# Moving the first products of an expert layer's dense loop ahead, so that blocks without one come last

## The chip, the core and the metric

The kernel runs on one core of one Trainium2 chip. A core has five engines that run side by side and wait for each other through semaphores: TensorE (PE, matrix products; PEld is its weight load), VectorE (DVE), ScalarE (ACT), GpSimd (POOL) and SyncE (SP, which here issues DMA transfers). The metric is device time in microseconds for one execution; lower is better. Each engine works through its own list of instructions strictly in the order in which it was written, so an instruction that waits holds up everything behind it on its engine.

## The reference, cut to what matters

Two layers, each a token mixer (attention in the first, pooling in the second) followed by an expert layer. Nearly two thirds of the time goes to the loops of the two expert layers:

```python
def _peer(h, w_q, k1, k2, u_tab, v_tab):             # h: 512 tokens x 1024; tables: 16384 x 1024
    q = (h @ w_q).reshape(b, l, 8, 2, 128)           # 8 heads, two half queries
    s1, s2 = q[..., 0, :] . k1, q[..., 1, :] . k2    # scores against 128 keys each
    v1, i1 = top_k(s1, 16);  v2, i2 = top_k(s2, 16)
    top_s, pos = top_k(v1 + v2 (all pairs), 16)      # 16 experts of 16384 per head
    idx = i1 * 128 + i2 at pos;  g = softmax(top_s)
    a = gelu(u_tab[idx] . h)                         # 128 experts per token
    return sum(g * a * v_tab[idx])
x = layernorm(alpha * x + gate * _peer(...))
```

## The kernel before, in words

The 512 tokens of an expert layer are treated in two ways. For the first 384 tokens (`TD`, three tiles of 128) the kernel works densely: it goes through all 16384 experts in 128 blocks of 128. For block b the **first product** (`u_block`, L950) multiplies the block's rows of `peer_u` with the tokens, 24 matmuls 384 columns wide into PSUM tile `pA` or `pG`, and ScalarE writes the Gelu of it to a strip `gel[b]`. VectorE multiplies that strip by the block's gates (`w_mul`, L1134, result `W`; the gate is zero where a token did not choose the expert), `w_hi` and `w_lo` split `W` into a rounded part `WH` and a rest `WL`, and the **second product** (`v_block`, L1152) multiplies it with the block's rows of `peer_v`, 18 matmuls 512 columns wide, summed over all blocks in the PSUM tiles `acc`. Each half row block of a table is one transfer of 256 KB on SyncE's queue (`fetch`, tile `raw`, 6 buffers), and ScalarE (`hi`) and VectorE (`lo`, L101) split it in two as well (`prep`), four halves ahead of TensorE.

For the last 128 tokens the kernel **gathers**: `g_fetch` has GpSimd fetch, for all 128 tokens at once, the row of their i-th chosen expert (an indirect DMA of 512 KB into one of four slots of the tile `flat`), 128 rows of `peer_u`, then 128 of `peer_v`. `g_step` (L1260) has VectorE multiply a row of `peer_u` with the tokens and sum it (L1267), or add a row of `peer_v` to the sum `accg` (L1277). Before this can start, the choice of experts for these tokens must be made: `late_route` (L1384) does it in steps, on VectorE (`top16_steps`, `look_one`) and GpSimd (`ranks`, sums of `look_one`, the list `idx`). It is a Python generator; each `next(late)` writes the instructions of one more step, and four groups of two heads are done one after the other.

Before the loop stands a stretch in which the gates of the 384 tokens are made, while TensorE makes the first products of blocks 0 to 25 (`PRE + 2`). The gates go to DRAM and come back four blocks at a time (`g_load`, tile `gb`, 3 buffers, 768 KB).

The order is written out by hand (no scheduler moves anything): the loop over b from L1447 on. In the kernel before, iteration b makes the first product of block b + 3 (`LEAD`) if that is at least 26, so iterations 0 to 22 hold a second product alone, iterations 23 to 124 both, 125 to 127 a second alone. The strips of blocks 0 to 23 lie in the upper part of `flat` (`A0`); later ones use two buffers `gel`. One step of `late_route` is written per iteration up to 21, three from 22 on. `spread_rows` (L853) is a small planner: from estimated costs per iteration it works out up to which gathered row (`goal`) VectorE shall be after each iteration, from iteration 22 to 120. `Fin` loads what the closing layer norm needs; `last` (iteration 123) does it for the gathered tokens, `turn` (iteration 125) transposes that result in the first layer.

Of the kernel before, what the change touches and what calls it, by code (L numbers as in the profile page):

```python
# [10 lines left out]
F32 = mybir.dt.float32  # L11
# [25 lines left out]
TD = ND * 128  # L37
# [4 lines left out]
KB = 4  # L42
PRE = 24
# [8 lines left out]
def body(ctx: ExitStack, tc, A):  # L52
    nc = tc.nc
# [796 lines left out]
        return rt  # L850


    def spread_rows(pre, lead, begin, end):  # L853

        spec = []
        for b in range(end):
            u = pre + 2 <= b + lead < 128
            spec.append((4.12 + 4.15 * u, 2.5 + 1.4 * u, 2.05 + 1.48 * u))
        u = 0.5
        while True:  # L860
            x = [max(0.0, min((u * p - n) / 1.25, (0.95 * p - d) / 1.47)) if b >= begin else 0.0
                 for b, (p, n, d) in enumerate(spec)]
            if sum(x) >= 2 * NSEL:
                break
            u += 0.005
        goal, t = [], 0.0
        for v in x:
            t += v
            goal.append(min(2 * NSEL, int(t)))
        goal[-1] = 2 * NSEL  # L870
        return goal + [2 * NSEL] * (128 - end)
# [18 lines left out]
    def peer(rt):  # L890
# [5 lines left out]
        d1 = Pool("dense1", side=Y)  # L896
# [15 lines left out]

        NB = 128
        LEAD = 3
        GEND = 121
        seq = [("U", b, k) for b in range(PRE + 2) for k in range(2)]
        for b in range(NB):
            u = b + LEAD
            if PRE + 2 <= u < NB:
                seq += [("U", u, 0), ("U", u, 1)]  # L920
            seq += [("V", b, 0), ("V", b, 1)]
        pos_of = {k: i for i, k in enumerate(seq)}
        raw, HL = {}, {}
# [21 lines left out]
        gel, WHL, Wt = {}, {}, {}  # L945
        A0 = flat[:, 3 * 128 * SG:].rearrange("p (b t) -> p b t", b=PRE)

        def u_block(b, hook=None):
            p = psU.tile([128, 512], F32, name="pG" if b % 2 else "pA")
            for k in range(2):  # L950
                i = pos_of["U", b, k]
                fetch(i + 6)
                prep(i + 4)
                h_, l_ = HL.pop(i)
                for c in range(4):
                    cc, w = 4 * k + c, slice(c * 128, (c + 1) * 128)
                    mm3(p[:, :TD], (h_[:, w], l_[:, w]), (hH[:, cc, :], hL[:, cc, :]), cc == 0, cc == DC - 1)
                if k == 0 and hook:
                    hook()
            if b < PRE:  # L960
                gel[b] = A0[:, b, :]
            else:
                gel[b] = d1.tile([128, TD], F32, name="gel", bufs=2)
            nc.scalar.activation(gel[b], p[:, :TD], AF.Gelu)


# [254 lines left out]
        def g_load(j, queue):  # L1221
            if j < NB // KB:
                gb[j] = d2.tile([128, NSG, KB * SG], F32, name="gb", bufs=3)
                queue.dma_start(gb[j].rearrange("p s (i t) -> p s i t", t=SG), gates[l][:, :, KB * j:KB * (j + 1), :])
# [7 lines left out]
        def hook():  # L1232
            due[0] += per
            while due[0] >= 1.0:
                due[0] -= 1.0
                next(pipe, None)
# [14 lines left out]
        def g_fetch(n):  # L1251
            while step["f"] < min(n, 2 * NSEL):
                i = step["f"]
                assert i >= NSEL or i < step["n"]
                r = flat[:, i % 4 * D:(i % 4 + 1) * D]
                nc.gpsimd.indirect_dma_start(out=r, out_offset=None,  # L1256
                                             in_=A["peer_u_rows"] if i < NSEL else A["peer_v_rows"],
                                             in_offset=bass.IndirectOffsetOnAxis(ap=idx[:, i % NSEL:i % NSEL + 1], axis=0))
                rows[i] = r
                step["f"] += 1  # L1260
# [122 lines left out]
        def late_route():  # L1383

            at = [4 * D]

            def space(shape, dt=F32):
                n = math.prod(shape) * (2 if dt == BF else 4) // 4
                w = flat[:, at[0]:at[0] + n]
                at[0] += n  # L1390
                if dt != F32:
                    w = w.bitcast(dt)
                names = "abcd"[:len(shape)]
                return w.rearrange(f"p ({' '.join(names)}) -> p {' '.join(names)}", **dict(zip(names, shape)))

            V3, I3, Ib3 = space((2 * H, TK)), space((2 * H, TK), U32), space((2 * H, TK), BF)
            cand, T3, P3, pu3 = space((H, NC_)), space((H, TK)), space((H, TK), U32), space((H, TK), U32)
            f3, ab3, ids3 = space((4, 5, 2 * TK)), space((4, 2, 2 * TK), BF), space((4, 2, 2 * TK))
            x3, e3 = space((2, H * TK, TK), BF), space((2, H * TK, TK), BF)
            s3, E3 = space((1, H)), space((H, TK))  # L1400
            V4, Ib4 = [w.rearrange("p (h k) i -> p h k i", k=2) for w in (V3, Ib3)]
            x4, e4 = [w.rearrange("p k (h i) j -> p k h i j", h=H) for w in (x3, e3)]
            for g in range(H // 2):
                hs, ks = slice(2 * g, 2 * g + 2), range(4 * g, 4 * g + 4)
                for i, _ in enumerate(top16_steps([(V3[:, k], I3[:, k], S3[:, k]) for k in ks])):
                    if i % 5 == 4:
                        yield
                nc.scalar.copy(Ib3[:, 4 * g:4 * g + 4], I3[:, 4 * g:4 * g + 4])
                for k in range(2):
                    nc.scalar.copy(x4[:, k, hs], Ib4[:, hs, k, :, None].to_broadcast([128, 2, TK, TK]))  # L1410
                candidates(cand[:, hs], V4[:, hs, 0], V4[:, hs, 1], 2)
                yield
                for i, _ in enumerate(top16_steps([(T3[:, k], P3[:, k], cand[:, k])
                                                   for k in range(2 * g, 2 * g + 2)])):
                    if i % 5 == 4:
                        yield
                f, ab, id_ = [w[:, g].rearrange("p a (h k) -> p a h k", h=2) for w in (f3, ab3, ids3)]
                ranks(ab, P3[:, hs], pu3[:, hs], f)
                yield
                for k in range(2):  # L1420
                    look_one(id_[:, k], e4[:, k, hs], ab[:, k], x4[:, k, hs], 2)
                yield
                r = f3[:, g, 0]
                nc.gpsimd.tensor_scalar(r, ids3[:, g, 0], 128.0, float(l * NEXP), op0=OP.mult, op1=OP.add)
                nc.gpsimd.tensor_tensor(r, r, ids3[:, g, 1], op=OP.add)
                nc.gpsimd.tensor_copy(idx[:, 2 * g * TK:2 * (g + 1) * TK], r)
                step["n"] += 2 * TK
            nc.vector.tensor_tensor(E3, T3, T3[:, :, 0:1].to_broadcast([128, H, TK]), op=OP.subtract)
            nc.scalar.activation(E3, E3, AF.Exp)
            yield  # L1430
            nc.vector.reduce_sum(s3[:, 0], E3, axis=AX.X)
            nc.vector.reciprocal(s3[:, 0], s3[:, 0])
            nc.vector.tensor_tensor(ga.rearrange("p (h k) -> p h k", h=H), E3,
                                    s3[:, 0, :, None].to_broadcast([128, H, TK]), op=OP.mult)
# [6 lines left out]
            w_lo(b)  # L1441
        w_mul(2)
        late = late_route()
        first = PRE - 2
        goal = spread_rows(PRE, LEAD, first, GEND)
        fin = None
        for b in range(NB):  # L1447
            u = b + LEAD
            if b + 2 < NB:
                w_hi(b + 2)  # L1450
            if PRE + 2 <= u < NB:
                u_block(u)
            if b + 2 < NB:
                w_lo(b + 2)
            v_block(b)
            if b + 3 < NB:
                w_mul(b + 3)
                if (b + 3) % KB == KB - 1:
                    g_load((b + 3) // KB + 3, nc.sync)
            for _ in range(1 if b < first else 3):  # L1460
                next(late, None)
            while step["i"] < goal[b]:
                g_step()
            if l == 0 and 97 <= b < 113 and b % 2:

                c = (b - 97) // 2
                nc.sync.dma_start(rows_at(c, 1)[:, 0, :], A["pool_w_in"][c * 128:(c + 1) * 128, :])
            if b == GEND + 1:
                gpp.close()
                fin = Fin()  # L1470
            if b == NB - 5:
                fin.last()
            if b == NB - 3:
                fin.turn()
# [4 lines left out]

    rt = mla()  # L1480
    rt = pool_mixer(peer(rt))
    fin = peer(rt)
    fin.finish()
# [76 lines left out]
```

## Time and profile before

| | us |
|---|---|
| median of 3 runs | 3115.03 (3106.61 to 3117.44) |
| the profiled execution, its own time | 3110.56 |
| its span in the trace | 3108.8 |
| TensorE busy / VectorE busy in the span | 2964.6 / 2403.7 |
| ScalarE busy / GpSimd busy in the span | 1237.0 / 990.2 |

The mean granted clock of TensorE in the profiled execution was 0.985 of full speed. The dense loop ran from about 666 to 1656 us in the first layer (the first pass) and from about 2101 to 3092 us in the second (the second pass). A row of a timeline reads: start, duration, engine, line, operation, written tile <- read tiles, shapes, and in brackets how long the engine had been idle before it and who released it. A row of waits reads: who waited, for whom, total us, times, longest. L96 and L97 are lines of a helper (`mm3`) that all large products share, so tiles tell them apart: `acc` is the second product, `pA` and `pG` the first.

### The profile page before, as it was taken

What the parts mean: (1) busy time and instruction counts of PE and PEld (TensorE: products, weight loads), DVE (VectorE), ACT (ScalarE), POOL (GpSimd) and SP (SyncE); (2) the same over time, 40 slices, a digit from 0 to 9 for tenths busy, and PEclk for the clock granted to TensorE, in tenths of its full rate; (3) what the DMA queues carried; (4) which work ended last, traced back from release to release, by engine and by line L of the source; (5) the groups of instructions that cost most, each with busy time, mean ns of one, the idle gap of its engine ahead of it and who ended that gap; (6) DMA issues with size and microseconds to landing.
All of it is one profiled execution on the core that took longest, in us unless ns stands there. A gap on an engine that the chain in (4) does not pass through costs nothing. (4 is left out here: it accounts for less than half of the span.)

```text
span 3108.8 us, 45004 instructions
## 1 busy us (share of the span) xinstructions
PE 2964.6 (95%) x15364; PEld 2518.5 (81%) x15364; DVE 2403.7 (77%) x4917; ACT 1237.0 (40%) x2271; POOL 990.2 (32%) x1051
## 2 busy tenths in 40 slices
PE   7999999999799999999998999899899999999997
PEld 4777657888699999989996756887789899988996
DVE  7777798977777877878865378987777787787886
ACT  3444334544333333333334334554333333333333
POOL 0000353003544444444312135002444344344441
PEclk9999999999899999999999999999999999999999
DMA  6367522775799989999962332575689999998993
GB/s 255 120 217 237 176 75 85 268 244 163 247 324 313 325 314 313 322 310 345 348 227 82 143 95 65 207 269 182 203 292 316 314 319 316 314 316 307 321 313 137
DMA packets 351479, 756.98 MB, mean 243 GB/s; under 512 B 30336, under 2 KB 121600, under 8 KB 347792
## 3 DMA queue, kind: packets, MB, share of 16 engines
q1 hardware_dynamic: 270768, 423.21, 40.3%
q0 software_dynamic: 77024, 280.56, 25.9%
q10 hardware_dynamic: 3456, 50.33, 4.2%
q8 instruction: 120, 1.97, 0.3%
q14 instruction: 111, 0.91, 0.1%
HBM read 695.26 MB, written 58.72 MB: 243 GB/s over the span
## 5 line engine op out<-in xcount | busy, mean ns | idle before, releaser
L101 DVE TENSOR_TENSOR lo<-raw,hi 128x512 fp32r<-128x512 f32 x1024 | 679.7, 698 | 344.2 <-ACT hi L100 343.7
L100 ACT CAST hi<-raw 128x512 fp32r<-128x512 f32 x1024 | 596.1, 617 | 144.3 <-DMA raw<-in_peer_uT_dram 83.7
L96 PE MATMUL acc<-lo,WH 128*128 128x512 f32 x1536 | 609.7, 397 | 43.8 <-DVE lo L101 43.8
L95 PE MATMUL acc<-hi,WH 128*128 128x512 f32 x1536 | 602.7, 392 | 9.9 <-ACT WH L1144 7.5
L97 PE MATMUL acc<-hi,WL 128*128 128x512 f32 x1536 | 607.1, 395 | 0.0
L1256 POOL DMA_INDIRECT flat<-in_peer_v_rows_dram,idx x256 | 339.0, 1324 | 472.0 <-DVE accg L1277 401.2
L1256 POOL DMA_INDIRECT flat<-in_peer_u_rows_dram,idx x256 | 338.6, 1323 | 442.0 <-DVE flat L1267 396.5
L96 PEld LDWEIGHTS acc<-lo,WH 128*128 128x128 f32 x1536 | 291.4, 190 | 109.0 <-DVE lo L101 52.4
L1144 ACT CAST WH<-W 128x384 fp32r<-128x384 f32 x256 | 131.5, 514 | 560.7 <-PE acc L96 390.9
L97 PE MATMUL pG<-hH,lo 128*128 128x384 f32 x1024 | 345.7, 338 | 8.0 <-DVE lo L101 7.8
L95 PE MATMUL pA<-hH,hi 128*128 128x384 f32 x1024 | 347.1, 339 | 1.6 <-ACT hi L100 1.6
L95 PE MATMUL pG<-hH,hi 128*128 128x384 f32 x1024 | 347.1, 339 | 0.0
L95 PEld LDWEIGHTS acc<-hi,WH 128*128 128x128 f32 x1536 | 291.3, 190 | 68.0 <-ACT WH L1144 8.2
L97 PE MATMUL pA<-hH,lo 128*128 128x384 f32 x1024 | 344.1, 336 | 0.2
L96 PE MATMUL pG<-hL,hi 128*128 128x384 f32 x1024 | 344.1, 336 | 0.0
L96 PE MATMUL pA<-hL,hi 128*128 128x384 f32 x1024 | 343.4, 335 | 0.0
L1277 DVE SCALAR_TENSOR_TENSOR accg<-flat,wa,accg 128x1024 f32<-128x1024 f32 x254 | 325.6, 1282 | 20.7 <-DMA flat<-in_peer_v_rows_dram,idx 15.4
L1267 DVE SCALAR_TENSOR_TENSOR flat<-flat,h2g 128x1024 f32<-128x1024 f32 x256 | 303.1, 1220 | 49.5 <-DMA flat<-in_peer_u_rows_dram,idx 49.4
L97 PEld LDWEIGHTS acc<-hi,WL 128*128 128x128 f32 x1536 | 291.7, 190 | 60.7
L97 PEld LDWEIGHTS pG<-hH,lo 128*128 128x128 f32 x1024 | 193.1, 189 | 9.9 <-DVE lo L101 9.9
L95 PEld LDWEIGHTS pA<-hH,hi 128*128 128x128 f32 x1024 | 193.2, 189 | 6.4 <-ACT hi L100 2.3
L91 PE MATMUL mm<-h2T,wq 128*128 128x512 f32 x448 | 196.9, 592 | 0.0
(375 smaller groups left out, 4400.9 us busy)
## 6 DMA issues: line engine op xcount, KB each, us to landing
raw<-in_peer_uT_dram SPq DMA_DIRECT2D x512, 256.0 KB, 6.1
raw<-in_peer_v_rows_dram SPq DMA_DIRECT2D x512, 256.0 KB, 6.4
gates<-flat ACTq DMA_DIRECT2D x24, 2048.0 KB, 7.3
gb<-gates SPq DMA_DIRECT2D x58, 768.0 KB, 5.5
wmod<-in_w_mod_dram SPq DMA_DIRECT2D x84, 512.0 KB, 4.4
wq<-in_peer_w_q_dram SPq DMA_DIRECT2D x32, 512.0 KB, 3.7
wo<-in_w_mod_dram SPq DMA_DIRECT2D x12, 512.0 KB, 5.1
gb<-gates POOLq DMA_DIRECT2D x6, 768.0 KB, 8.2
```

Source lines behind the costliest of these rows:

```text
L91: nc.tensor.matmul(out, lhsT, rhs, start=first, stop=last)
L95: nc.tensor.matmul(out, a[0], b[0], start=first, stop=False)
L96: nc.tensor.matmul(out, a[0], b[1], start=False, stop=False)
L97: nc.tensor.matmul(out, a[1], b[0], start=False, stop=last)
L100: nc.scalar.copy(hi, src)
L101: nc.vector.tensor_tensor(lo, src, hi.bitcast(F32), op=OP.subtract)
L1144: nc.scalar.copy(wh, Wt[b])
L1256: nc.gpsimd.indirect_dma_start(out=r, out_offset=None, in_=A["peer_u_rows"] if i < NSEL else A["peer_v_rows"], in_offset=bass.IndirectOffs ...
L1267: nc.vector.scalar_tensor_tensor(r, r, 1.0, h2g, op0=OP.mult, op1=OP.mult, accum_out=aa[:, i:i + 1])
L1277: nc.vector.scalar_tensor_tensor(accg[0], r, wa[:, k:k + 1], accg[0], op0=OP.mult, op1=OP.add)
```

## The change

Iteration b now makes the first product of block 26 + b, for b from 0 to 101; iterations 102 to 127 hold a second product alone. The strips are 26 in a ring (`turns`: 24 in `A0` and two tiles), the new one written where block b's own stood. Three steps of `late_route` are written per iteration in iterations 0 to 14, none later; the planner is told of them and places gathered rows from iteration 15 to 117. An empty step stands between `ranks` and `look_one`, and the first four rows are fetched as soon as the first group's list is there. A gate load is written two iterations later than before.

```diff
-        GEND = 121
+        GEND = 118
         seq = [("U", b, k) for b in range(PRE + 2) for k in range(2)]
+
+        news = []
         for b in range(NB):
-            u = b + LEAD
-            if PRE + 2 <= u < NB:
-                seq += [("U", u, 0), ("U", u, 1)]
+            news.append([PRE + 2 + b] if PRE + 2 + b < NB else [])
+            seq += [("U", u, k) for u in news[b] for k in range(2)]
             seq += [("V", b, 0), ("V", b, 1)]
...
+        turns = [A0[:, i, :] for i in (2, 3, 4, 5, *range(10, PRE), 6, 7, 8, 9)]
+        turns[-2:] = [*[d1.tile([128, TD], F32, name=f"gel{k}") for k in range(2)], *turns[-2:]]
+        turns += [A0[:, i, :] for i in (0, 1)]
...
-            if b < PRE:
-                gel[b] = A0[:, b, :]
-            else:
-                gel[b] = d1.tile([128, TD], F32, name="gel", bufs=2)
+            gel[b] = turns[b % (PRE + 2)]
...
                 ranks(ab, P3[:, hs], pu3[:, hs], f)
                 yield
+                yield
                 for k in range(2):
                     look_one(id_[:, k], e4[:, k, hs], ab[:, k], x4[:, k, hs], 2)
...
                 step["n"] += 2 * TK
+                g_fetch(4)
...
-        first = PRE - 2
-        goal = spread_rows(PRE, LEAD, first, GEND)
+        steps = [3] * 15 + [0] * NB
+        goal = spread_rows(news, steps, 15, GEND)
         fin = None
         for b in range(NB):
-            u = b + LEAD
             if b + 2 < NB:
                 w_hi(b + 2)
-            if PRE + 2 <= u < NB:
+            for u in news[b]:
                 u_block(u)
...
-                if (b + 3) % KB == KB - 1:
-                    g_load((b + 3) // KB + 3, nc.sync)
-            for _ in range(1 if b < first else 3):
+                if b + 3 >= KB and (b + 3) % KB == 1:
+                    g_load((b + 3) // KB + 2, nc.sync)
+            for _ in range(steps[b]):
                 next(late, None)
```

What stood on TensorE where the loop begins, the end of block 25's first product (`pG`) and block 0's second (`acc`), in the kernel before:

```order
L95 MATMUL pG<-hH,hi 128x384
L96 MATMUL pG<-hL,hi 128x384
L97 MATMUL pG<-hH,lo 128x384
L95 MATMUL acc_4296<-hi,WH 128x512
L96 MATMUL acc_4296<-lo,WH 128x512
L97 MATMUL acc_4296<-hi,WL 128x512
```

What stands there now, the same end of block 25 and then the beginning of block 26's first product (`pA`):

```order
L95 MATMUL pG<-hH,hi 128x384
L96 MATMUL pG<-hL,hi 128x384
L97 MATMUL pG<-hH,lo 128x384
L95 MATMUL pA<-hH,hi 128x384
L96 MATMUL pA<-hL,hi 128x384
L97 MATMUL pA<-hH,lo 128x384
```

Block 0's second product now stands 24 matmuls later.

On VectorE, before, iteration 23 held the third group's look-up (L1022, L1024), the next step of top-16 (MAX, MAX_INDEX) and the first gathered rows (L1267), all ahead of iteration 24's splits (`lo`):

```order
L1006 TENSOR_SCALAR flat<-flat 128x32
L1022 TENSOR_TENSOR flat<-flat,rep 128x512
L1024 TENSOR_TENSOR flat<-flat 128x512
L1022 TENSOR_TENSOR flat<-flat,rep 128x512
L1024 TENSOR_TENSOR flat<-flat 128x512
L879 MAX flat<-S_4291 128x8 x4
L883 MAX_INDEX flat<-flat,S_4291 128x8
L1267 SCALAR_TENSOR_TENSOR flat,aa<-flat,h2g 128x1024 x3
L101 TENSOR_TENSOR lo<-raw,hi 128x512 x2
L1149 TENSOR_TENSOR WL<-W,WH 128x384
```

Now the last instructions of the routing (L1435 to L1437, the softmax) stand in iteration 13, and the first gathered rows (L1269 now) at the end of iteration 15:

```order
L1435 TENSOR_REDUCE flat<-flat 128x8
L1436 RECIPROCAL flat<-flat 128x8
L1437 TENSOR_TENSOR ga__3013<-flat 128x128
L101 TENSOR_TENSOR lo<-raw,hi 128x512 x2
L1151 TENSOR_TENSOR WL<-W,WH 128x384
L101 TENSOR_TENSOR lo<-raw,hi 128x512 x2
L1139 TENSOR_TENSOR W<-flat,gb 128x384
L101 TENSOR_TENSOR lo<-raw,hi 128x512 x2
L1151 TENSOR_TENSOR WL<-W,WH 128x384
L101 TENSOR_TENSOR lo<-raw,hi 128x512 x2
L1139 TENSOR_TENSOR W<-flat,gb 128x384
L1269 SCALAR_TENSOR_TENSOR flat,aa<-flat,h2g 128x1024 x2
```

Routing and gathered rows no longer share an iteration. On GpSimd, before, after the third group's list (L1426) eleven row fetches stood ahead of the fourth group's `ranks` (L1009):

```order
L1424 TENSOR_SCALAR flat<-flat 128x32
L1425 TENSOR_TENSOR flat<-flat 128x32
L1426 CAST idx<-flat 128x32
L1256 DMA flat<-in_peer_u_rows_dram,idx 128x1024 x11
L1009 CAST flat<-flat 128x32
L1010 CAST flat<-flat 128x32
```

Now four fetches stand behind the first group's list, and the other 124 of that table behind the fourth's:

```order
L1427 TENSOR_SCALAR flat<-flat 128x32
L1428 TENSOR_TENSOR flat<-flat 128x32
L1429 CAST idx<-flat 128x32
L1258 DMA flat<-in_peer_u_rows_dram,idx 128x1024 x4
L1011 CAST flat<-flat 128x32
L1012 CAST flat<-flat 128x32
```

None of these four has to wait for VectorE to consume a row first.

## Rows read from the trace of the kernel before

**Rows 1.** The page, busy time, share of the span and instructions by engine.

```profile
PE 2964.6 (95%) x15364; PEld 2518.5 (81%) x15364; DVE 2403.7 (77%) x4917; ACT 1237.0 (40%) x2271; POOL 990.2 (32%) x1051
```

**Rows 2.** Busy us by stretch and engine (x is instructions), first pass's loop.

```profile
core 0: us, PE busy (x) PEld busy (x) DVE busy (x) ACT busy (x) POOL busy (x), PEclk, DMA share, GB/s
667.00:762.00 95.00, 95.00 (x416) 78.55 (x415) 78.26 (x244) 41.49 (x80) 22.29 (x44) 0.99 0.59 187
762.00:859.00 97.00, 77.47 (x365) 68.34 (x364) 68.54 (x174) 31.34 (x59) 50.70 (x69) 0.89 0.68 226
859.00:1190.00 331.00, 330.68 (x1672) 300.73 (x1671) 259.27 (x450) 125.28 (x239) 140.71 (x105) 1.00 0.92 318
1190.00:1590.00 400.00, 399.45 (x2020) 362.96 (x2019) 325.53 (x419) 152.16 (x289) 164.99 (x127) 1.00 0.93 327
```

**Rows 3.** Timeline of ScalarE, the 1st and 9th Gelu of each pass's loop.

```profile
766.12 0.49 ACT L964 ACTIVATE gel<-pA 128x384 f32<-128x384 f32 x1 [2.86 <-PE pA L97]
858.20 0.49 ACT L964 ACTIVATE gel<-pA 128x384 f32<-128x384 f32 x1 [2.00 <-PE pA L97]
2202.13 0.49 ACT L964 ACTIVATE gel<-pA 128x384 f32<-128x384 f32 x1 [2.86 <-PE pA L97]
2294.87 0.49 ACT L964 ACTIVATE gel<-pA 128x384 f32<-128x384 f32 x1 [2.85 <-PE pA L97]
```

**Rows 4.** Timeline of all engines around the first gathered row.

```profile
778.12 1.11 POOL L1256 DMA_INDIRECT flat<-in_peer_u_rows_dram,idx  x1 [0.17 <-issue]
782.53 1.23 DVE L1267 SCALAR_TENSOR_TENSOR flat<-flat,h2g 128x1024 f32<-128x1024 f32 x1 [7.18 <-DMA flat<-in_peer_u_rows_dram,idx]
788.30 0.79 PE L96 MATMUL acc<-lo,WH 128*128 128x512 f32 x1 [11.61 <-DVE lo L101]
```

**Rows 5.** Waits of all engines from 762 to 859 us.

```profile
engine line waited for: us in total, times, longest us
PE acc L96 <- DVE lo L101: 18.3, 3, 11.6
POOL flat L1009 <- DVE flat L883: 14.8, 1, 14.8
DVE flat L1022 <- POOL flat L1018: 6.5, 2, 3.3
```

**Rows 6.** Timeline where the loop begins, each pass.

```profile
665.06 0.56 DVE L1137 TENSOR_TENSOR W<-flat,gb 128x384 f32<-128x384 f32 x1 [4.55 <-DMA gb<-gates]
666.22 0.79 PE L95 MATMUL acc<-hi,WH 128*128 128x512 f32 x1 [3.91 <-ACT WH L1144]
2101.28 0.80 PE L95 MATMUL acc<-hi,WH 128*128 128x512 f32 x1 [3.64 <-ACT WH L1144]
```

**Rows 7.** Instructions by line and shape, VectorE from 667 to 762 us.

```profile
L101 DVE TENSOR_TENSOR lo<-raw,hi 128x512 fp32r<-128x512 f32 x46 | 30.9, 703 | 6.0 <-ACT hi L100 6.0
L1149 DVE TENSOR_TENSOR WL<-W,WH 128x384 fp32r<-128x384 f32 x24 | 13.7, 570 | 9.2 <-ACT WH L1144 9.1
L1137 DVE TENSOR_TENSOR W<-flat,gb 128x384 f32<-128x384 f32 x23 | 13.5, 585 | 0.0
```

**Rows 8.** The page, instructions by line, rows gathered for the second table.

```profile
L1277 DVE SCALAR_TENSOR_TENSOR accg<-flat,wa,accg 128x1024 f32<-128x1024 f32 x254 | 325.6, 1282 | 20.7 <-DMA flat<-in_peer_v_rows_dram,idx 15.4
```

**Rows 9.** Busy time by stretch, one slice of 10 us.

```profile
1510.00:1520.00 10.00, 10.00 (x51) 8.96 (x50) 8.24 (x12) 3.17 (x7) 3.02 (x3) 1.00 1.03 407
```

**Rows 10.** Waits of the DMA queue of SyncE, whole span.

```profile
SPq L1224 <- DVE W L1137: 393.5, 48, 13.9
```

**Rows 11.** Timeline of VectorE, GpSimd and TensorE at a pass's end.

```profile
1628.53 1.22 DVE L124 TENSOR_TENSOR nr<-accg,flat 128x1024 f32<-128x1024 f32 x1
1635.53 4.86 DVE L101 TENSOR_TENSOR lo<-raw,hi 128x512 fp32r<-128x512 f32 x2 [2.24 <-ACT hi L100]
1634.65 2.38 POOL L142 TENSOR_TENSOR xo<-nr,flat 128x1024 f32<-128x1024 f32 x1 [45.99 <-DMA flat<-x_mid]
1637.64 0.50 PE L96 MATMUL acc<-lo,WH 128*128 128x512 f32 x1 [1.24 <-DVE lo L101]
```

More of the change, by code (lines that the diff above doesn't have):

```diff
@@ L850, in pool_mixer, with spread_rows @@
         return rt
-    def spread_rows(pre, lead, begin, end):
+    def spread_rows(news, late, begin, end):
         spec = []
         for b in range(end):
-            u = pre + 2 <= b + lead < 128
-            spec.append((4.12 + 4.15 * u, 2.5 + 1.4 * u, 2.05 + 1.48 * u))
+            u = len(news[b])
+            spec.append((4.12 + 4.15 * u, 2.5 + 1.4 * u + 1.45 * late[b], 2.05 + 1.48 * u))
         u = 0.5
```

## The prediction

> **What bounds the kernel now.** I read the page's first part, then busy time by stretch, then the waits and the timeline where TensorE is not full. TensorE is the bound: busy 2964.6 of 3108.8 us [rows 1]. In the first pass's loop it is full in three of the four long stretches: from 667 to 762 us (second products alone) it is busy 95.00 of 95, with 416 matmuls, 0.228 us each, so 18 x 0.228 = 4.11 us a block; from 859 to 1190 us (both products and gathered rows) 330.68 of 331, with 1672 matmuls, 0.198 each, so 42 x 0.198 = 8.31 us a block [rows 2]. A first product is thus worth 4.20 us. Only the stretch between, 762 to 859 us, is not full: 77.47 of 97, at a granted clock of 0.89 [rows 2]. The loop makes 128 second and 102 first products before and after, so its full-speed time does not change. What can change is the time lost beside it.
>
> How much is lost there is read from the Gelus, one for each first product: the first begins at 766.12 us, the ninth at 858.20, and in the second pass 2202.13 and 2294.87 [rows 3]. Eight blocks at 8.31 are 66.5 us; they took 92.1 and 92.7. **Lost: 25.6 and 26.2 us.**
>
> Why: VectorE, which makes the splits `lo` that TensorE needs, stood still on the first gathered row. The list of experts came so late that the fetch was issued only at 778.12; VectorE, in iteration 23, idled 7.18 us for the row, until 782.53, did three rows, and only then came to the splits, which TensorE had awaited 11.61 us [rows 4]; its first matmul behind that took 0.79 us, about twice what it takes at full speed, so the idle time also cost clock. Two more waits of the same kind make 18.3 us in all [rows 5]. They come from routing and rows taking turns: the fourth group's `ranks` (L1009) idled 14.8 us of GpSimd's time behind a VectorE that was held up by rows, and `look_one` (L1022) waited 6.5 us for GpSimd, since it stands right behind `ranks` in the same iteration [rows 5].
>
> A smaller loss stands where each loop begins: `W` waits 4.55 us for gates that come back from DRAM, and TensorE idles 3.91 us in the first pass and 3.64 in the second [rows 6].
>
> **The change part by part.** The sum is made against the profiled execution's 3110.56 us, which is 4.5 below the median of the three runs and inside their range.
>
> *Start of the loop.* Block 26's first product, whose four halves are split in the stretch before, now stands ahead of block 0's second. It takes 4.2 us and needs no gates, so it covers 3.91 and 3.64. The first blocks behind such an idle stretch also ran at a lower clock; I count 1 us a pass for that (bounds 0 and 2). Gain: 7.5 + 2 = 9.5 us.
>
> *Routing and rows taken apart.* All routing now lies in iterations 0 to 14, and the first four rows are fetched in iteration 3, twelve iterations (some 100 us) before VectorE wants them. The wait of 7.18 us goes, and no row stands between two steps. Gain if all of it goes: 25.6 + 26.2 = 51.8 us. What is late next would be VectorE itself in those 15 iterations. Its load: from 859 to 1190 us it is busy 259.27 us in 331 / 8.31 = 39.8 blocks, 6.5 a block; of this 2.64 rows at 1.28 us, as those of the second table take [rows 8], which leaves 3.1. A routing step: from 667 to 762 us VectorE is busy 78.26 us in 23.1 blocks, each with one step [rows 2]; splits, `W` and `WL` are 30.9 + 13.7 + 13.5 of it [rows 7], and the rest, 20.2 us, is 0.9 us a step. Three steps and a block with both products are 3.1 + 2.7 = 5.8 of 8.31 us; if the three steps that meet cost twice the mean, 8.5. VectorE is up to one block ahead, so I count 1 us a pass for such places and for the one group (the third) whose `look_one` still stands in the iteration of its `ranks` (bounds 0 and 10 a pass). Cost: 2 us.
>
> *Rows with both products.* The planner's numbers go from 2.64 to 2.80 rows a block. That is 0.2 us more of VectorE, 6.7 of 8.31, and 0.16 x 0.524 MB / 8.31 us = 10 GB/s more on 318 and 327 [rows 2]. A slice of 10 us with 407 GB/s shows TensorE full all the same [rows 9]. Cost 0, at most 3.
>
> *Second products alone, with rows.* Iterations 102 to 117 now carry one row each (13 rows are left at 102, the planner gives 0.95 per iteration). VectorE: two splits at 0.703, `WL` 0.570, `W` 0.585 [rows 7] and a row at 1.28 make 3.8 of 4.11 us; a wait for a row was rare, 20.7 us over 254 [rows 8]. It fits, with little to spare; and the stretch from 667 to 762 us was as full with a routing step of 0.9 in the row's place. Cost: between 0 and 1 us for each of the 13 rows, so 0 to 13 a pass; I take 0, the end that the full stretch of rows 2 is nearest to.
>
> *Gate loads.* Before, SyncE's queue stood 393.5 us behind `W` for a gate buffer [rows 10], with the raw loads queued behind. Two iterations later the buffer is free when the load's turn comes. TensorE did not wait for it from 667 to 762 us, so this is worth nothing by itself; the load still comes seven iterations (29 us at least) ahead of its use.
>
> *End of the pass.* `last` now stands among blocks of 4.11 us, before among blocks of 8.31. From its first instruction at 1628.53 to the end of the splits behind it (1635.53 + 4.86) VectorE delivers nothing for 11.9 us; the two splits took 4.86 because they ran beside GpSimd's 2.38 us operation, and TensorE waited 1.24 [rows 11]. Now TensorE has three blocks, 12.3 us, less what is used up when `last` begins, some 2 to 3 us. Cost 3 us a pass (bounds 0 and 7); 6 us. Loads of the closing norm (`Fin`) wait in the first pass for strips that are freed only in iteration 118, with raw loads behind them on the queue: 1 us (0 to 4).
>
> **Sum:** 3110.56 - 9.5 - 51.8 + 2 + 0 + 6 + 1 = **3058 us**, 1.7% less. Everything at its good end gives 3048, everything at its bad end 3118, which I do not expect at once.
>
> **A rule that speaks against it.** Rows 11 show two splits at 2.4 us each beside an operation of GpSimd. The Trainium skill ("SBUF — State Buffer", Who interferes with whom) says that a VectorE instruction with two SBUF inputs and a GpSimd instruction that reads SBUF share a port, and that the one which comes first blocks the other for its whole length. The end of the pass agrees; the routing stretch agrees only weakly, a split there took 703 ns [rows 7].
>
> **Rivals.** (1) *GpSimd's routing work blocks VectorE.* GpSimd was busy 22.29 us while two groups were routed [rows 2], so 45 us a pass, 3 us for each of the 15 iterations. If all of it were added, VectorE would need 8.8 of 8.31 us on average, and 11.5 in the fullest iterations: 7 to 20 us lost a pass, time 3072 to 3098. Against it: 703 ns a split. Chance 0.06. (2) *Rows among second products alone do not fit.* Each of them costs 1 us: 13 a pass, time 3084. For it: 3.8 of 4.11 us. Chance 0.08. (3) *Slower: the steps themselves were what cost the time.* In the stretch that lost 25.9 us, 16 of the 38 steps stood, 1.6 us lost a step. If that belongs to steps beside first products and not to rows, 38 steps in 15 iterations lose 61 a pass; time 3058 - 2 + 122 = 3178. It is slower from 0.72 us a step on (54.6 us over 76 steps). For it: both products and three steps an iteration is just what that stretch had. Against it: the longest wait of VectorE there is for a row, and one step in 4.11 us cost nothing. Chance 0.04. (4) *The hole only moves.* The first rows, four slots and nothing more, stall VectorE at iteration 15 as before, and the loop loses 20 us a pass there: 3098 or, with clock and the end of the pass, near 3110. Against it: the slots are full by then. Chance 0.03.
>
> **How the numbers follow.** The forecast has 0.79; (1) to (4) have 0.06, 0.08, 0.04 and 0.03. The forecast's own range is 3042 to 3076 (the good end less what runs differ; the middle of the costs). To leave out no more than 2 in 10 and to take in (2), the range is 3042 to 3088. A difference of 0.3%, about 9 us, is what a measurement of this kernel can tell from none. Faster: forecast, (1), (2), half of (4), 0.94; same: 0.02; slower: 0.04.
>
> **What would show it.** In the profile after: TensorE busy without a hole from the start of the loop to block 101, Gelus 8.3 us apart from the first on; no wait of VectorE for the first row; L1024 waiting for GpSimd at most once a pass for some 3 us; the first second product right behind a first one, without the idle 3.9; SyncE no longer behind `W`. The end of the loop should show 1 to 4 us of TensorE waiting for `lo` around `last`. The forecast is wrong if TensorE waits for `lo` in many of the first 15 iterations (1 or 3), or in iterations 102 to 117 (2).

## The result, and the profile after

The changed kernel takes 3058.05 us (median of 4 runs, 3057.72 to 3058.78), the kernel before 3115.14 beside it: a ratio of 0.9825, 95% interval 0.9811 to 0.984. The forecast was 3058. Its sum was made against one profiled execution; there the time went from 3110.56 to 3058.78 and the span from 3108.8 to 3057.0, 51.8 us less, where the terms of the sum give 52.3.

Busy time by stretch of the changed kernel, columns as in [rows 2]:

```profile
core 0: us, PE busy (x) PEld busy (x) DVE busy (x) ACT busy (x) POOL busy (x), PEclk, DMA share, GB/s
667.00:762.00 95.00, 92.18 (x463) 82.84 (x462) 71.22 (x255) 40.14 (x80) 33.20 (x70) 1.00 0.60 189
762.00:859.00 97.00, 97.00 (x491) 88.12 (x490) 73.32 (x158) 39.40 (x75) 34.77 (x41) 1.00 0.75 246
859.00:1190.00 331.00, 331.00 (x1677) 301.46 (x1676) 267.50 (x462) 123.33 (x241) 143.32 (x112) 1.00 0.96 327
1500.00:1640.00 140.00, 133.86 (x581) 108.00 (x580) 101.41 (x149) 51.51 (x96) 29.56 (x21) 0.98 0.70 246
```

The stretch from 762 to 859 us, 77.47 busy at a clock of 0.89 before, is full at 1.00. What is left stands in the first row and the last. The waits from 762 to 859 us, to set beside [rows 5]:

```profile
POOL flat L1011 <- DVE flat L883: 15.0, 1, 15.0
DVE flat L1269 <- DMA flat<-in_peer_u_rows_dram,idx: 1.9, 2, 1.1
```

TensorE is not in that list any more. GpSimd's `ranks` still waits 15.0 us for VectorE's top-16, and no engine waits for GpSimd in this stretch. VectorE's 7.18 us for the first row [rows 4] have become 1.9 in all. From 667 to 762 us one row of that list answers to the 6.5 us of `look_one`:

```profile
DVE flat L1024 <- POOL flat L1020: 3.2, 1, 3.2
```

The begin of the first pass's loop, to set beside [rows 6], the issue of the gate loads first:

```profile
660.94 3.17 POOL L1226 DMA_DIRECT2D gb<-gates  x3 [145.19 <-DMA raw<-in_peer_v_rows_dram]
668.80 0.56 DVE L1139 TENSOR_TENSOR W<-flat,gb 128x384 f32<-128x384 f32 x1 [6.16 <-DMA gb<-gates]
669.96 0.50 PE L95 MATMUL acc<-hi,WH 128*128 128x512 f32 x1 [1.36 <-ACT WH L1146]
673.68 0.50 PE L95 MATMUL acc<-hi,WH 128*128 128x512 f32 x1 [1.24 <-ACT hi L100]
```

TensorE no longer idles 3.91 us at once, but it idles twice: for the gates, in spite of the first product put ahead of them, and then for the second half of block 0, whose `hi` ScalarE makes only behind the first `WH`.

The end of the first pass's loop, to set beside [rows 11]:

```profile
1611.63 2.39 POOL L142 TENSOR_TENSOR xo<-nr,flat 128x1024 f32<-128x1024 f32 x1 [55.84 <-ACT nr L137]
1611.98 2.46 DVE L1151 TENSOR_TENSOR WL<-W,WH 128x384 fp32r<-128x384 f32 x1 [1.71 <-ACT WH L1146]
1614.10 2.54 POOL L143 TENSOR_TENSOR xo<-xo,flat 128x1024 f32<-128x1024 f32 x1
1614.37 3.42 DVE L101 TENSOR_TENSOR lo<-raw,hi 128x512 fp32r<-128x512 f32 x2
1617.24 0.79 PE L96 MATMUL acc<-lo,WH 128*128 128x512 f32 x1 [3.87 <-DVE lo L101]
```

Each VectorE row begins beside a GpSimd row and ends soon after that one ends. TensorE waits 3.87 us for it (1.24 before). By stretch, the clock is the third column from the right:

```profile
1580.00:1612.00 32.00, 31.32 (x143) 25.81 (x142) 17.90 (x32) 13.69 (x25) 0.37 (x1) 1.00 0.51 166
1612.00:1618.00 6.00, 2.13 (x9) 1.46 (x8) 6.00 (x4) 0.99 (x2) 5.19 (x3) 0.81 0.61 242
1618.00:1622.00 4.00, 3.87 (x12) 2.68 (x10) 2.07 (x4) 1.64 (x4) 0.00 (x0) 0.50 0.32 131
```

So the wait also costs some 2 us of clock, an estimate from the last row: 3.87 of 4 us busy at half of full speed.

SyncE's 393.5 us behind `W` [rows 10] are gone; its queue waits for free raw buffers instead:

```profile
SPq L932 <- DVE lo L101: 1671.6, 910, 14.0
```

**Where the time went.** From the starts of the matmuls I worked out what each part of a loop loses: each distance to the next start, less 0.2286 us behind a matmul of a second product and 0.1742 behind one of a first, added up over a part and both passes. Each kernel was traced once, so its row holds for that one execution.

| us lost, both passes | begin to block 21 | blocks 22–39 | blocks 40–117 | blocks 118–127 |
|---|---|---|---|---|
| before | 10.6 | 53.0 | 6.5 | 11.0 |
| after | 8.2 | 0.4 | 0.2 | 17.8 |
| gained | 2.4 | 52.6 | 6.3 | −6.8 |

The sum is 54.5. The span fell by 51.8, so 2.7 us were lost outside the loops, mostly ahead of the first (that stretch took 661.0 to 666.0 us in kernels that have the same code there, so I read nothing from it).

The two constants are not quite right. Blocks 1 to 21 have no wait that counts, and yet they read -0.034 us a block before (second products alone) and +0.011 after (both products). With that taken out the four gains are 4.3, 52.7, 4.8 and -7.4. Block 0 alone, where the begin is lost, goes from 12.1 to 7.8 us.

### The profile page after: what moved, and what is told of

It reads as the page before. It is cut to its first block, busy times and chain, and to the rows that moved or that the text cites. A ratio compares the mean times of both kernels' runs of the same rounds, so it can differ in the third digit from the quotient of the medians.

```text
span 3057.0 us, 44994 instructions
## 1 busy us (share of the span) xinstructions
PE 2950.0 (96%) x15364; PEld 2511.6 (82%) x15364; DVE 2403.4 (79%) x4917; ACT 1215.1 (40%) x2267; POOL 968.7 (32%) x1051
## 4 chain that ended last, share of the span: by engine, by line
PE 82%; DVE 10%; issue 4%; DMA 2%; ACT 2%; POOL 0%; SPq 0%; ACTq 0%; DVEq 0%; POOLq 0%
PE acc L96 11%; PE acc L97 11%; PE acc L95 11%; PE mm L91 7%; PE pA L95 5%; PE pA L97 5%; PE pG L97 5%; PE pA L96 5%; PE pG L95 5%; PE pG L96 5%; DVE lo L101 2%; DVE eq L1192 2%; DVE oh L1187 2%; PE po L91 1%; PE y L96 1%
## 5 line engine op out<-in xcount | busy, mean ns | idle before, releaser
L96 PE MATMUL acc<-lo,WH 128*128 128x512 f32 x1536 | 603.2, 393 | 8.2 <-DVE lo L101 8.2
L100 ACT CAST hi<-raw 128x512 fp32r<-128x512 f32 x1024 | 585.4, 617 | 16.9 <-DMA raw<-in_peer_v_rows_dram 4.8
L1258 POOL DMA_INDIRECT flat<-in_peer_u_rows_dram,idx x256 | 330.8, 1292 | 437.6 <-DVE flat L1269 384.4
L1269 DVE SCALAR_TENSOR_TENSOR flat<-flat,h2g 128x1024 f32<-128x1024 f32 x256 | 304.5, 1222 | 29.6 <-DMA flat<-in_peer_u_rows_dram,idx 29.2
```

The lines of the kernel that those rows point to most:

```text
L96: nc.tensor.matmul(out, a[0], b[1], start=False, stop=False)
L100: nc.scalar.copy(hi, src)
L1258: nc.gpsimd.indirect_dma_start(out=r, out_offset=None, in_=A["peer_u_rows"] if i < NSEL else A["peer_v_rows"], in_offset=bass.IndirectOffs ...
L1269: nc.vector.scalar_tensor_tensor(r, r, 1.0, h2g, op0=OP.mult, op1=OP.mult, accum_out=aa[:, i:i + 1])
```

## The experiments

**Taking turns, or something beside it?** The first kernel puts routing and rows back into the same iterations and leaves the rest of the change; the second does the routing early in the old order of products.

e4_mixed, from the changed kernel:

```diff
         goal = spread_rows(news, steps, 15, GEND)
+        steps = [0] * 9 + steps
```

> The changed kernel with the routing moved nine iterations later: three steps an iteration in iterations 9 to 23, gathered rows from 15 as now. Routing and rows take turns again in nine iterations, but the first rows are still fetched early and the empty step is there. My theory (taking turns costs by itself: ranks behind fetches on GpSimd, and 6.7 + 2.7 us of VectorE in 8.31): 10 to 26 us a pass lost, 3078 to 3110. Rival (only the late first fetch cost, taking turns is free): 3058 to 3064.

Measured: 3105.1 us, ratio 0.9974 (0.9963 to 0.9985): 47 us of the gain are gone. The loops lose 35.6 us up to block 21 and 21.9 from there to 39. By stretch, the first pass:

```profile
680.00:762.00 82.00, 82.00 (x417) 74.65 (x416) 39.40 (x91) 30.75 (x60) 0.00 (x0) 1.00 0.52 161
762.00:859.00 97.00, 87.63 (x420) 78.44 (x419) 78.98 (x252) 34.90 (x69) 52.78 (x84) 0.95 0.61 205
```

With the steps among the rows the hole is back in the same place, though first products stand as in the changed kernel. The order of the products alone, with late gate loads in it, gives 8 us. The kernel does not split the cause further: the planner did not know of the moved steps, and from 800 to 830 us VectorE is busy 28.23 of 30 us (21.55 before), so here too much work for VectorE does part of what its waits did in the kernel before.

e3_split_only, from the kernel before:

```diff
                 ranks(ab, P3[:, hs], pu3[:, hs], f)
                 yield
+                yield
...
                 step["n"] += 2 * TK
+                g_fetch(4)
...
-            for _ in range(1 if b < first else 3):
+            for _ in range(2 if b < 21 else 0):
```

> The kernel before, with its order of products and its gate loads, but the routing written two steps an iteration in iterations 0 to 20, so that it is over before the first gathered row, with the empty step and the early fetch of four rows. My theory: the 52 us of iterations 22 to 40 go, and VectorE pays for two steps beside a second product alone (2.55 + 1.8 = 4.35 of 4.11 us, 5 to 10 us a pass): 3070 to 3085. Rival (first products must stand beside the routing for the gain): 3100 to 3120, since what is saved at the rows is lost in iterations 0 to 20.

Measured: 3080.78 us, ratio 0.9889 (0.9867 to 0.9912). The hole is gone (3.0 us lost in blocks 22 to 39), but 27.9 are lost ahead of it, 17 more than before. There TensorE makes second products alone, and two steps an iteration are close to too much for VectorE, 71.77 busy of 82 us:

```profile
680.00:762.00 82.00, 78.96 (x341) 63.01 (x340) 71.77 (x261) 35.57 (x68) 39.49 (x81) 1.00 0.56 181
```

So the old order holds the routing only at a price; first products put ahead make the room, some 8.3 us an iteration. This is what the reordering is worth: not time of its own, but room for three steps. (This kernel keeps the early gate loads; the old order with the routing early and the gate loads late was not run.)

e5_no_early_fetch, from the changed kernel:

```diff
                 step["n"] += 2 * TK
-                g_fetch(4)
```

> The changed kernel without the early fetch of the first four rows: they are fetched when the first row is wanted, in iteration 15. Theory that the late first fetch is a large part of what was lost: VectorE idles 4 to 7 us there as before, and with one block of lead TensorE loses 0 to 6 us a pass: 3060 to 3070. Rival (with the routing over by then, the lead of VectorE covers it): 3056 to 3060.

Measured: 3060.74 us, ratio 0.9829 (0.9813 to 0.9845): not told apart from the changed kernel. The time lies at the edge of the theory's range, so the trace decides, and it is for the rival: the first fetch is issued at 790.34 instead of 708.37 us, and yet VectorE waits no longer for rows than in the changed kernel (1.9 us in both from 762 to 859 us; 2.9 and 2.5 from 680 to 880). The late fetch of [rows 4] was late because the list was; to fetch early adds nothing once the routing is done in time.

**The gate loads.** One kernel takes this edit back, one makes it alone, one takes it back and adds a raw buffer.

e1_gates_early, from the changed kernel:

```diff
-                if b + 3 >= KB and (b + 3) % KB == 1:
-                    g_load((b + 3) // KB + 2, nc.sync)
+                if (b + 3) % KB == KB - 1:
+                    g_load((b + 3) // KB + 3, nc.sync)
```

> The changed kernel with the gate loads written two iterations earlier, as they were before. My theory (the time came from routing and gathered rows no longer taking turns on VectorE and GpSimd): 3058 to 3064 us, since TensorE did not wait while SyncE stood behind W; the queue of SyncE stands some 390 us behind W again. Rival (the raw loads that stood behind a waiting gate load were the cause): 3100 to 3115.

Measured: 3087.24 us, ratio 0.9911 (0.988 to 0.9943). The edit is worth 29 us, half of the whole gain, which neither theory had. The loss is 28.8 us in blocks 40 to 117 instead of 0.2. SyncE's queue in this kernel, and ScalarE's `hi` from 1050 to 1560 us with its idle time ahead of it and what ended that:

```profile
SPq L1226 <- DVE W L1139: 415.0, 52, 15.7
```

```profile
L100 ACT CAST hi<-raw 128x512 fp32r<-128x512 f32 x239 | 140.8, 618 | 84.7 <-DMA raw<-in_peer_uT_dram 48.9 <-DMA raw<-in_peer_v_rows_dram 33.8 <-ACT flat L966 0.6
```

The same row in the changed kernel:

```profile
L100 ACT CAST hi<-raw 128x512 fp32r<-128x512 f32 x246 | 140.3, 617 | 7.3 <-DMA raw<-in_peer_v_rows_dram 4.8 <-DMA raw<-in_peer_uT_dram 2.5
```

A gate load that waits for its buffer holds the raw loads behind it on the queue; they land late, `hi` and `lo` come late. That the queue is the cause, and not slower transfers, is read by setting each raw load beside the `hi` that reads it: in this stretch ScalarE waited for all 15 halves whose load was issued right behind a gate load, 42.3 us together, half of its idle time for halves, though `hi` began 7.6 us behind the issue in the median; in the changed kernel it waited for 2 of 17, and `hi` began 9.7 us behind the issue. So the loads were issued late, and TensorE is no longer full in a stretch where both kernels do the same work (e1_gates_early first, the changed kernel below):

```profile
1050.00:1500.00 450.00, 444.78 (x2232) 400.52 (x2232) 363.22 (x512) 169.19 (x320) 194.86 (x148) 1.00 0.94 321
1500.00:1600.00 100.00, 96.02 (x425) 79.28 (x424) 77.54 (x111) 37.38 (x70) 29.71 (x20) 0.98 0.88 309
```

```profile
1050.00:1500.00 450.00, 450.00 (x2278) 409.82 (x2277) 372.43 (x522) 168.29 (x328) 196.56 (x152) 1.00 0.96 330
1500.00:1600.00 100.00, 99.32 (x452) 83.28 (x451) 76.14 (x114) 38.78 (x75) 22.51 (x17) 1.00 0.89 311
```

e2_gates_late_only, from the kernel before: the same lines the other way.

```diff
-                if (b + 3) % KB == KB - 1:
-                    g_load((b + 3) // KB + 3, nc.sync)
+                if b + 3 >= KB and (b + 3) % KB == 1:
+                    g_load((b + 3) // KB + 2, nc.sync)
```

> The kernel before with the gate loads alone written two iterations later. My theory: 3109 to 3115 us; it can take away at most the few us that the kernel before lost in single blocks behind block 40 (6 us in both passes). Rival (the queue of SyncE was the cause): 3060 to 3075.

Measured: 3114.17 us, ratio 0.9996 (0.9985 to 1.0006). In the old order the edit gives 4.8 us in blocks 40 to 117 and loses 8.3 at the two begins (18.9 instead of 10.6): nothing. Alone, the gate loads are worth nothing and the rest of the change 25.5 us (e1_gates_early against the kernel before beside it); together they are worth 57.

e9_7raw, from e1_gates_early:

```diff
-                r = d1.tile([128, 512], F32, name="raw", bufs=6)
+                r = d1.tile([128, 512], F32, name="raw", bufs=7)
...
-                fetch(i + 6)
+                fetch(i + 7)
```

> The kernel of e1_gates_early (changed order, gate loads as early as before) with seven raw buffers in place of six, fetched one half further ahead. My theory after e1 (SyncE stands behind W with raw loads queued behind, so halves land late): ScalarE's waits for raw halves fall and one to two thirds of the 29 us come back: 3067 to 3078. Rival (an earlier gate load takes DMA time from the rows or halves of the moment, and no queue matters): 3084 to 3090.

Measured: 3066.06 us, ratio 0.9846 (0.9827 to 0.9865): 21 of the 29 us come back, a little more than the theory had, though SyncE waits as long as in e1_gates_early. TensorE is full again in the first of the two stretches:

```profile
SPq L1226 <- DVE W L1139: 426.2, 52, 9.0
```

```profile
1050.00:1500.00 450.00, 450.00 (x2276) 409.58 (x2275) 372.62 (x522) 168.78 (x327) 195.07 (x151) 1.00 0.94 330
```

One more raw buffer covers the wait. It is thus the lateness of the raw halves that costs, and not the gates. (A further buffer would cover halves that are late for any reason; that the queue makes them late is read from the issues above.)

**The begin of the loop.** e6_splits_first and e12_start ask what is left there, e10_one_gate_first is one half of the latter.

e6_splits_first, from the changed kernel:

```diff
+        prep(st["prep"] + 2)
         for b in range(2):
             w_mul(b)
```

> The changed kernel, with two more second-factor halves split ahead, in ScalarE's and VectorE's order in front of the loop's first two gate products, so that V0,1 and one more stand ready when V0 begins. Theory A (what is left at the loop's begin in the changed kernel, 3.8 and 4.0 us, is in part TensorE waiting 1.24 us for ScalarE's hi of V0,1 and the pieces of clock behind it, the rest the wait for the gates): that wait goes, 1.2 to 2 us a pass come back, median 3055.0 to 3057.5. Theory B (the split merely moves: it stands on ScalarE ahead of WH and pushes the first wait by its own 0.6 to 1.3 us): median 3057.5 to 3060.

Measured: 3055.08 us, ratio 0.9822 (0.9804 to 0.984). By the times it can't be told from the changed kernel; the trace tells: up to block 21 the loops lose 4.0 us instead of 8.2 (with the same begin as the changed kernel, e5, e7 and e13 lose 8.8, 11.6 and 10.3 there, so single traces differ by some 3 us). Of TensorE's waits for `acc` from 640 to 690 us one belongs to the loop:

```profile
PE acc L95 <- ACT WH L1146: 1.7, 1, 1.7
```

The wait for `hi` is gone (theory A).

e10_one_gate_first, from the changed kernel:

```diff
-        for j in range(3):
-            g_load(j, nc.gpsimd)
+        g_load(0, nc.gpsimd)
         for b in range(2):
             w_mul(b)
             w_hi(b)
+            g_load(b + 1, nc.scalar)
             w_lo(b)
```

> The changed kernel with only the first of the three gate loads issued ahead of the loop; the second and third are issued by ScalarE behind the first two WH. My theory of the start (the first gates land late, 7.9 us after their issue, because three gate loads and raw loads share the DMA engines): the first W comes 2 to 4 us earlier and the idle 1.4 us goes: 2 to 5 us in both passes, 3053 to 3056. Rival (latency of the store and load alone): no change, 3057 to 3059.

Measured: 3056.45 us, ratio 0.9814 (0.9798 to 0.983). The first `W` begins 8.2 us behind the issue of its load (667.14 and 658.99), in the changed kernel 7.9 (6.9 and 7.5 in the second pass): two loads fewer in flight do not bring the 2 to 4 us of the theory. The time lies between the two ranges.

e12_start: both edits.

> The changed kernel with both edits to the loop's begin: the extra splits ahead of the first gate products, and only the first of the three gate loads issued by GpSimd in front of the loop, the other two by ScalarE behind the first two WH. Theory A (the first gates come late because the three loads and the raw loads share the same engines; fewer bytes in flight bring the first piece sooner): first W 1 to 3 us earlier than in the changed kernel, the start loses 1 to 2 us instead of 4, median 3051 to 3055. Theory B (the first gates' time of some 8 us is the store's and load's own latency, not a matter of bytes): the first W comes no sooner, the edit is worth only what the extra splits give, median 3054.5 to 3057.

Measured: 3053.02 us, ratio 0.9808 (0.9791 to 0.9824); first `W` 8.6 us behind its load's issue, 7.0 us lost up to block 21. Theory A falls, since its first `W` was to come 1 to 3 us earlier. The median lies a little under B's range; the traced execution is the slowest of the four (3056.2 us), so its trace does not say where the median's gain came from.

**The end of the loop.** e7_affine_late was to move GpSimd's two operations behind the loop, by writing L142 and L143 of the third token tile behind it:

```diff
                 xn = norm_end(self.wk, self.x.pop(t), self.r.pop(t))
+                if t == 3:
+                    if l == 0:
+                        self.load(1)
+                    return xn
...
+            def out3(self):
+                dst = x_out[:, 3, :] if l == 0 else A["out"][384:512, :]
+                affine(self.wk, self.xn, self.ln, dst, (nc.gpsimd, nc.gpsimd))
+
             def rest(self):
+                self.out3()
```

(and a call at the same place in `finish`.)

> The changed kernel with GpSimd's two operations of last (the affine part of the norm of the gathered tokens, and its store) written behind the loop. If the two splits of 4.9 us beside them are what TensorE waits 3.9 us for at the end of each pass, that wait falls to 0 to 1 us and the splits take 1.3: 3050 to 3055, if the work behind the loop hides the two operations; 3056 to 3062 if it does not. If VectorE's own norm work is what TensorE waits for, the wait stays above 3 us: 3057 to 3062.

Measured: 3058.85 us, ratio 0.982 (0.9804 to 0.9837), no change, but the experiment missed its aim:

```profile
1609.83 2.39 POOL L142 TENSOR_TENSOR xo<-nr,flat 128x1024 f32<-128x1024 f32 x1 [58.31 <-ACT nr L137]
1610.18 2.46 DVE L1151 TENSOR_TENSOR WL<-W,WH 128x384 fp32r<-128x384 f32 x1 [1.71 <-ACT WH L1146]
```

GpSimd has nothing else to do there, so the operation starts as soon as `nr` is there, wherever it is written. It tells nothing of the two theories. e13_affine_vector is the same edit with `(nc.vector, nc.vector)` for the engines, which does hold the two operations back, behind VectorE's last split.

> The changed kernel with the two 128x1024 operations that scale and shift the third token tile's normalised rows moved from GpSimd, where they run from 1611.6 to 1616.6 in the first pass, to VectorE behind the loop's last block (L142 and L143). Theory A (WL at 2.46 us and a pair of lo at 3.42 us, against 0.55 and 1.29 elsewhere, are slow because GpSimd's two operations run beside them; that makes the 3.87 us wait of TensorE and, behind it, the granted clock of 0.50 in 1618 to 1622): with GpSimd idle there, WL takes 0.55, the pair 1.3, the wait is under 1 us, the clock stays 1.00, and 4 to 6 us a pass come back, less up to 2 us where VectorE's two operations stand in the way of the end: median 3047 to 3053. Theory B (VectorE is slow there for another reason, such as the raw halves landing or ScalarE's hi that the lo reads): durations and wait as they were, median 3057 to 3062.

Measured: 3048.81 us, ratio 0.9802 (0.9785 to 0.9819). The place of the five rows above:

```profile
1610.33 0.56 DVE L1151 TENSOR_TENSOR WL<-W,WH 128x384 fp32r<-128x384 f32 x1 [1.71 <-ACT WH L1146]
1610.85 1.29 DVE L101 TENSOR_TENSOR lo<-raw,hi 128x512 fp32r<-128x512 f32 x2
1618.32 1.22 DVE L142 TENSOR_TENSOR xo<-nr,flat 128x1024 f32<-128x1024 f32 x1
1619.57 1.23 DVE L143 TENSOR_TENSOR xo<-xo,flat 128x1024 f32<-128x1024 f32 x1
```

```profile
1612.00:1618.00 6.00, 4.40 (x24) 3.52 (x23) 4.00 (x10) 3.49 (x8) 0.00 (x0) 1.00 0.35 146
1618.00:1622.00 4.00, 4.00 (x19) 3.16 (x18) 3.92 (x5) 0.00 (x0) 0.60 (x1) 1.00 0.00 0
```

`WL` takes 0.56 us instead of 2.46, the pair of `lo` 1.29 instead of 3.42, TensorE does not wait for them, and the clock stays at 1.00. The ends lose 6.9 us instead of 17.8, less than the kernel before (11.0). Theory A is shown.

e14_all_three: the edits of e12_start and e13_affine_vector.

> The changed kernel with the three edits together: the extra splits and one gate load first at the loop's begin, and the scale and shift of the third tile's rows on VectorE behind the loop. If the places are apart, the gains add: with 0 to 4 us at the begins and 6 to 10 us at the ends, median 3044 to 3052; if the ends' operations on VectorE cost what they give, 3053 to 3057.

Measured: **3042.09 us** (3040.3 to 3044.87), ratio 0.9776 (0.9761 to 0.979), below the changed kernel's interval and a little under the range. The begins lose 4.2 us and the ends 6.9: the gains add (by the medians 5.0 and 9.2 us below the changed kernel alone, 16.0 together). It is the fastest kernel of the study.

## Why the prediction was right, and where its steps were not

*Routing and rows apart*, predicted 51.8 less 2: 52.6 in blocks 22 to 39, and only 0.23 us a pass is lost between blocks 1 and 21, where three steps an iteration stand. The cause was the one named, routing and rows in the same iterations: e4_mixed, which changes nothing but the iterations in which the steps stand, brings the loss back, though there in part by too much work for VectorE.

*Start of the loop*, predicted 9.5: 2.4 by the table, 4.3 with the constants put right. As kernels with the same begin lose 7.8 to 11.1 us in block 0 from one execution to another, where the kernel before lost 12.1, the term is worth some 1 to 4 us. This is the step that was mis-sized. It held that block 26's first product, 4.2 us, "needs no gates, so it covers 3.91 and 3.64". It covered the wait for the gates but for 1.4 us, since the first `W` came 7.9 us behind the issue instead of the 6.2 of the kernel before; and I forgot the second half of block 0, whose split was ready while TensorE idled 3.9 us and no longer is. In the three kernels that make that split ahead (e6_splits_first, e12_start, e14_all_three) the wait of 1.24 us is gone in both passes; they lose 4.0, 7.0 and 4.2 us up to block 21. Why the gates land later is not shown to the end, but all traces go one way. In the kernel before and e3_split_only SyncE issued no raw load between the issue of the first gate load and the first `W`, because its queue stood behind a waiting gate load, and `W` came 5.8 to 6.3 us behind the issue. In all others one to four raw loads of 256 KB were issued in that time, and it took 6.9 to 9.9 us. e2_gates_late_only, with later gate loads as its only edit, is among these (9.6 us), and two gate loads fewer in flight did not help.

*Gate loads*, "worth nothing by itself": true in the old order (e2_gates_late_only), wrong in the new one, where without it 29 us go. The step argued from a stretch, 667 to 762 us, with no gathered row in it and little else on the DMA engines (a share of 0.59), and took it for blocks in which rows and raw loads together reach 0.96. That the total held is luck here: the edit happened to be part of the change, and it took away a loss that the prediction did not see coming. The gain in blocks 40 to 117, 6.3 us by the table and 4.8 with the constants put right, is the part of it that the kernel before was already losing; e2_gates_late_only gains the same 4.8 there.

*Rows with both products*, 0, and *second products alone with rows*, 0: TensorE is busy 331.00 of 331 us in the first, and nothing is lost in blocks 102 to 117. VectorE's 3.8 of 4.11 us are enough, as long as the raw halves are on time: in e1_gates_early 13.3 of the 28.8 us are lost in these 16 blocks. (By the planner's list the 13 rows stand in iterations 102 to 114, not one in each up to 117.)

*End of the pass*, 6 and 1: 6.8. The size is right. Of its cause, the splits beside GpSimd's operation were named; e13_affine_vector shows that these, and not the 11.9 us in which VectorE is busy with `last`, are nearly all of it.

*The total*, 52.3 forecast and 51.8 measured from trace to trace, agrees better than its terms: the begin gave 5 us less than counted and 2.7 were lost outside the loops, while the gate loads gave 4.8 that were counted as nothing and routing and rows some 3 more. The median fell by 57.1 us, since the execution on which the sum stands was 4.5 us faster than the median before. The mechanism of the main term was right; that 3058 was hit to the microsecond is luck. (Everything at its good end adds up to 3047, not 3048.)

*The rivals.* (1) GpSimd's routing work does not block VectorE to a degree that matters: a split takes 712 ns from 680 to 800 us of the changed kernel, 703 before, and TensorE waits for nothing there. The rule on the shared port ("SBUF — State Buffer", Who interferes with whom, in the Trainium skill) stands all the same at the end of the pass, where e13_affine_vector agrees with it: 2.46 us beside GpSimd's operation, 0.56 alone. (2) No row among second products costs time. (3) Steps beside first products cost nothing; in e3_split_only, two of them in an iteration of 4.11 us do. (4) The hole did not move: 1.9 us of waits for the first rows, which TensorE did not feel.

## What to carry to other kernels

When the engine that feeds the bound engine does two kinds of work in turns, and one of them waits for data that the other produces, do the first kind to its end while there is slack; reorder the bound engine's own work to make that slack. An edit that is worth nothing in the old order can carry half the gain in the new one, so undo each edit in the *new* kernel to price it. An operation on an engine that is idle there starts when its data is there, as in e7_affine_late, wherever it is written; to move it in time, give it to an engine whose queue holds it.

## What the runs showed of the hardware that was not expected

VectorE's `WL`, with two inputs in SBUF, took 2.46 us beside GpSimd's operation of 2.39 us and 0.56 without it. It began 0.35 us behind that operation and ended 0.4 us behind its end (1614.44 behind 1614.02), as if it had waited for nearly the whole of it. In the stretch in which TensorE idled 3.87 us, 1612 to 1618, its granted clock read 0.81, and in the four microseconds behind it, 1618 to 1622, 0.50 of full speed, its level of 1.2 GHz; after idle times of 1.36 and 1.24 us at the loop's begin it read 1.00 over the stretch. A load that waits for a buffer holds later loads of SyncE's queue: 52 gate loads waited 415.0 us in all, and 29 us of the kernel's time went with it.
